# A hybrid Fourier and attention layer on one core: Fourier spectra kept as high and low part, modulation weights fetched two steps ahead, gate pieces between the blocks of the first q

## The chip, the cores and the metric

The kernel runs on 1 core of one Trainium2 chip. The metric is the device time in microseconds (us); a lower number is better. "Before" is the kernel without the change, "after" is the kernel with it. The engines are PE (TensorE, matrix products and transposes), DVE (VectorE), ACT (ScalarE), POOL (GpSimd) and SP (SyncE, which issues most of the DMAs).

## The reference, cut to what matters

One layer for 128 context tokens and 1024 latent tokens: a modulated norm, one input projection whose columns feed three users (a 2-D Fourier transform, windowed attention and two gates), a gated sum, an output projection, then a modulated squared-ReLU MLP. The modulation vectors are a matrix product of their own with `w_ada` (1024 x 6144).

```python
def modulation(cvec, w_ada, b_ada):
    m = jax.nn.silu(cvec) @ w_ada + b_ada
    return [t[:, None, :] for t in jnp.split(m, 6, axis=-1)]

def fourier_mix(u):
    ug = u.astype(jnp.float32).reshape(b, s, N_FOURIER_GROUPS, FOURIER_GROUP_DIM)
    f = jnp.fft.fft2(ug, axes=(1, 3), norm="ortho").real
    return f.reshape(b, s, FOURIER_WIDTH)

def merge_branches(u_f, attn_o, g, w_fo, w_ao, w_out):
    gates = jax.nn.sigmoid(g)
    g_f, g_a = gates[..., :D_MODEL], gates[..., D_MODEL:]
    m = g_f * (fourier_mix(u_f) @ w_fo) + g_a * (attn_o @ w_ao)
    return m @ w_out

def latent_layer(...):
    sh1, sc1, ga1, sh2, sc2, ga2 = mod
    h = rmsnorm(x, g1) * (1 + sc1) + sh1
    u_f, q, k, v, g = split_projection(h, w_in)
    q, k = rope(q), rope(k)
    attn_o = latent_attention(q, k, v, k_ctx, v_ctx, sink)
    x = x + ga1 * merge_branches(u_f, attn_o, g, w_fo, w_ao, w_out)
    h = rmsnorm(x, g2) * (1 + sc2) + sh2
    return x + ga2 * (jnp.square(jax.nn.relu(h @ w_ff1)) @ w_ff2)
```

## The kernel before, in words

Every float32 product is made of three matmuls on a high and a low part of its operands (`mm3`, L192 to L194): high x high, high x low, low x high. A weight block therefore goes three ways before PE can use it: a DMA loads it raw (`wraw`, two buffers), ACT casts the high part (`whi`, three buffers, L144) and DVE subtracts to get the low part (`wlo`, three buffers, L139, a helper line that every subtraction of this kind shares).

The stages, by their place in the span: norm, first modulation and the Fourier input u (to about 120 us); the Fourier transform of the four channel groups, with gate products as filler (to 185); the K and V projection of token tiles 0 to 5 (`tok_proj_round`, L230 to L232, to 210.6); the query projection of the first attention group, `q_pieces(0)`, six pieces of 24 matmuls (to 245); K and V of tiles 6 to 8 (to 258); 36 attention units, four groups of nine 128-token blocks (to about 707); the rest of the Fourier output product (to 729.6); the attention output product `w_ao` with the gated sum (to about 880); the output projection, the second norm and the MLP (to the end).

**Order.** From the K and V projection to the end of attention the order of PE is written out by hand. There PE alternates between attention work (scores `s` L758/L759, transposes `ptp` L792, values `o` L807/L808) and "fill": gate pieces, the query pieces of the next group and three pieces of the Fourier output product (`f_piece`, L929, L950), cut into sub-steps of a few matmuls. `fill_to` spreads the sub-steps evenly over the units. The order on the other engines and in SP's queue is made by a scheduler from the order of the program.

**Banks and buffers.** The fill has two PSUM banks (`mm`), the scores two (`s`), the values one (`o`). A piece of q leaves its bank by two DVE multiplies (L634/L635 for the even half, L637/L638 for the odd half), then DVE rotates (L639, L640), splits, and four stores per block go to `q_d`. The four `qt` tiles have one buffer each, so the multiplies of the next block wait for these stores. A gate piece leaves its bank by one ACT copy to `z` (L661) and one store to `z_d`. The values leave their bank by two ACT copies (`ot`, L816) and two DVE adds (`at`, L817).

**Modulation steps.** The later modulation blocks are worked off in small steps beside all this (`mod_step`). A step loads 128 x 256 of `w_ada` (`mraw`, three buffers, L305), scales it twice on ACT (`mprod`, one buffer, L309) and adds it on POOL (`macc`, L311, 70 times). A block has eight such steps and two more with transposes and sums on DVE (L327, L328); a small matmul with four DVE adds ends it (`mod_fold`, L274, L278). When the block of the first gate vector is complete, `ga_rows` (L1109) stores its columns to DRAM, 4 bytes at a time.

**Fourier output.** The transform stage stores each spectrum raw to `f_d`. At the start of the second last fill piece `load_fx` (L858 to L876) loads the four spectra and the edge rows, and ACT and DVE split them. `load_wfo` (L880 to L892) loads a block of `w_fo` and makes sums (L888) and differences (L889).

## Time and profile before

| | |
|---|---|
| time, median of 3 runs | 1673.37 us (1672.55 to 1673.9) |
| time of the profiled execution | 1677.22 us |
| its span, first to last instruction | 1675.4 us |
| mean granted TensorE clock | 0.993 |
| PE busy | 1618.5 us (97%) |
| DVE busy | 1146.0 us (68%) |
| ACT busy | 902.7 us (54%) |
| POOL busy | 271.4 us (16%) |

The profiled execution took 3.85 us more than the median, and 1.82 us of it lie outside its span. A time stamp in a row of the trace counts from the start of the span. A row reads: start, duration, engine, line, operation, output from inputs, shape; in brackets stands how long the engine was idle before it and what ended this wait. In the rows by stretch each engine has its busy time with the number of its instructions behind it, in the order PE, weight loads, DVE, ACT, POOL, then the granted clock, the busy share of the DMA engines and GB/s.

### The profile page before, as it was taken

What the parts mean: (1) busy time and instruction counts of PE and PEld (TensorE: products, weight loads), DVE (VectorE), ACT (ScalarE), POOL (GpSimd) and SP (SyncE); (2) the same over time, 40 slices, a digit from 0 to 9 for tenths busy, and PEclk for the clock granted to TensorE, in tenths of its full rate; (3) what the DMA queues carried; (4) which work ended last, traced back from release to release, by engine and by line L of the source; (5) the groups of instructions that cost most, each with busy time, mean ns of one, the idle gap of its engine ahead of it and who ended that gap; (6) DMA issues with size and microseconds to landing.
All of it is one profiled execution on the core that took longest, in us unless ns stands there. A gap on an engine that the chain in (4) does not pass through costs nothing.

```text
span 1675.4 us, 24835 instructions
## 1 busy us (share of the span) xinstructions
PE 1618.5 (97%) x8421; PEld 1423.5 (85%) x8421; DVE 1146.0 (68%) x2180; ACT 902.7 (54%) x1743; POOL 271.4 (16%) x368
## 2 busy tenths in 40 slices
PE   6999989998999999899999999999999999999998
PEld 5799888998899999789987888888888888888887
DVE  7653286866767766778648876777776588776764
ACT  7743356776777666455346654444444354444542
POOL 1010243444454333200002400000000100000000
PEclk9999999999999999999999999999999999999999
DMA  8342468555453332498465434544555996656751
GB/s 317 128 131 72 149 209 222 146 91 142 136 142 100 109 93 66 125 298 268 133 214 189 151 106 171 170 151 146 175 143 160 332 377 193 201 189 189 252 162 63
DMA packets 221135, 285.40 MB, mean 170 GB/s; under 512 B 30968, under 2 KB 148664, under 8 KB 220880
## 3 DMA queue, kind: packets, MB, share of 16 engines
q1 hardware_dynamic: 212752, 273.85, 52.0%
q0 software_dynamic: 8256, 9.96, 2.4%
q8 instruction: 66, 1.08, 0.3%
q14 instruction: 61, 0.50, 0.1%
HBM read 205.87 MB, written 77.88 MB: 169 GB/s over the span
## 4 chain that ended last, share of the span: by engine, by line
PE 72%; DVE 5%; DMA 3%; issue 2%; ACT 2%; POOL 1%; SPq 1%; DVEq 0%; ACTq 0%; POOLq 0%
PE x L1848 6%; PE x L1847 6%; PE x L1846 6%; PE x L1450 6%; PE x L1451 6%; PE x L1452 6%; PE mm L192 4%; PE mm L194 4%; PE mm L193 4%; PE ptp L792 2%; PE x L194 2%; PE x L192 2%; PE x L193 2%; PE s L758 2%; PE s L759 2%
## 5 line engine op out<-in xcount | busy, mean ns | idle before, releaser
L139 DVE TENSOR_TENSOR wlo<-wraw,whi 128x1024 fp32r<-128x1024 f32 x109 | 139.3, 1280 | 93.5 <-ACT whi L144 93.3
L144 ACT CAST whi<-wraw 128x1024 fp32r<-128x1024 f32 x107 | 111.8, 1048 | 81.1 <-DMA wraw<-in_w_ff_dram 17.7
L770 ACT ACTIVATE pt<-pt,mx 128x513 f32<-128x513 f32 (+2 forms) x144 | 95.8, 665 | 77.2 <-DVE mx L760 70.6
L193 PE MATMUL mm<-BR,whi 128*128 128x384 f32 x408 | 137.1, 336 | 0.0
L192 PE MATMUL mm<-BR,whi 128*128 128x384 f32 x360 | 129.1, 359 | 4.6 <-DVE qt L635 3.8
L1847 PE MATMUL x<-BR 128*128 128x512 f32 (+1 forms) x348 | 132.9, 382 | 0.0
L1848 PE MATMUL x<-BR 128*128 128x512 f32 (+1 forms) x348 | 132.5, 382 | 0.0
L1846 PE MATMUL x<-BR 128*128 128x512 f32 (+1 forms) x348 | 131.4, 382 | 0.0
L782 POOL TENSOR_SCALAR pt<-pt,mx 128x512 f32<-128x512 f32 (+2 forms) x144 | 97.1, 686 | 184.0 <-DVE mx L780 180.9
L760 DVE CUSTOM_DVE_ANT_0 pt<-s,mask,nsink 128x512 f32<-128x512 f32 (+2 forms) x144 | 96.4, 672 | 42.5 <-PE s L759 40.0
L194 PE MATMUL mm<-BR,wlo 128*128 128x384 f32 x360 | 121.3, 337 | 0.0
L1819 ACT CAST BR<-aa 128x512 fp32r<-128x512 f32 x80 | 49.7, 622 | 105.8 <-PE x L1847 51.3
L311 POOL TENSOR_TENSOR macc<-macc,mprod 128x512 f32<-128x512 f32 x70 | 93.5, 1335 | 40.4 <-ACT mprod L309 32.8
L139 DVE TENSOR_TENSOR pl<-ptp,ph 128x512 fp32r<-128x512 f32 x124 | 83.1, 686 | 19.0 <-ACT ph L795 17.6
L1450 PE MATMUL x<-BR,whi 128*128 128x512 f32 (+2 forms) x204 | 79.3, 389 | 4.1 <-ACT ZR L1474 2.8
L193 PEld LDWEIGHTS mm<-BR,whi 128*128 128x128 f32 x408 | 77.3, 190 | 6.3
L309 ACT ACTIVATE mprod<-mraw,siluc 128x256 f32<-128x256 f32 x140 | 63.8, 504 | 31.6 <-POOL macc L311 27.3
L139 DVE TENSOR_TENSOR BR<-aa,BR 128x512 fp32r<-128x512 f32 x80 | 55.0, 687 | 34.8 <-ACT BR L1819 34.3
L192 PEld LDWEIGHTS mm<-BR,whi 128*128 128x128 f32 x360 | 68.0, 189 | 11.8 <-DVE qt L635 4.4
L1452 PE MATMUL x<-BR,wlo 128*128 128x512 f32 (+2 forms) x204 | 78.0, 383 | 0.0
L1451 PE MATMUL x<-BR,whi 128*128 128x512 f32 (+2 forms) x204 | 78.0, 382 | 0.0
L792 PE MATMUL ptp<-ident,pt 128*128 128x128 f32 x496 | 74.0, 273 | 3.2 <-DVE pl L139 3.2
(450 smaller groups left out, 4758.5 us busy)
## 6 DMA issues: line engine op xcount, KB each, us to landing
aa<-hr_d SPq DMA_DIRECT2D x108, 256.0 KB
ab<-in_w_ff_dram SPq DMA_DIRECT2D x108, 256.0 KB
hr_d<-ZR SPq DMA_DIRECT2D x104, 256.0 KB
wraw<-in_w_in_dram SPq DMA_DIRECT2D x41, 512.0 KB
wraw<-in_w_ff_dram SPq DMA_DIRECT2D x34, 512.0 KB
mraw<-in_w_ada_dram SPq DMA_DIRECT2D x96, 128.0 KB
wraw<-in_w_out_dram SPq DMA_DIRECT2D x24, 512.0 KB
z_d<-z SPq DMA_DIRECT2D x48, 192.0 KB
```

The source lines that it names most:

```text
L139: eng.tensor_tensor(dst, raw, hi.bitcast(F32), ALU.subtract)
L144: nc.scalar.copy(hi, raw)
L192: nc.tensor.matmul(out, ah, bh, start=start, stop=False)
L193: nc.tensor.matmul(out, ah, bl, start=False, stop=False)
L194: return nc.tensor.matmul(out, al, bh, start=False, stop=stop).ins
L792: nc.tensor.transpose(pst[:, h * P : (h + 1) * P], u["pts"][h // 2][:, h % 2, b * P : (b + 1) * P], ident)
L1450: nc.tensor.matmul(po, wh, xh, start=(k == 0 and not cont), stop=False, skip_group_check=cont)
L1451: nc.tensor.matmul(po, wh, xl, start=False, stop=False, skip_group_check=cont)
L1452: nc.tensor.matmul(po, wl, xh, start=False, stop=(k == 3), skip_group_check=cont)
L1846: nc.tensor.matmul(ps, xh, bh, start=start, stop=False, skip_group_check=cont)
L1847: nc.tensor.matmul(ps, xh, bl, start=False, stop=False, skip_group_check=cont)
L1848: nc.tensor.matmul(ps, xl, bh, start=False, stop=stop, skip_group_check=cont)
```

## The change

The change does these things:

1. The transform stage splits each spectrum on the spot and stores high and low part (`f_d` has twice the size). `load_fx` loads both parts straight into their slots: eight DMAs, no cast, no subtraction. The edge rows of `w_fo` are split in the transform stage too and go through `wex_d`; the matmul of the edge rows has 12 rows and no longer 96.
2. The raw weights of modulation steps are loaded two steps ahead in the K and V projection and in attention (`mod_raw`, `raw_ahead`), with four buffers in place of three; `mprod` has two buffers in place of one; `z` has two in place of three.
3. Two gate pieces are taken out of the fill of attention and put behind the second and the fourth piece of the first q (`front`). The fill of attention has 53 pieces in place of 55 and is 16 sub-steps (48 matmuls) shorter.
4. Weight blocks in attention follow a plan (`at`): raw load 16 sub-steps before the piece that needs them, split 8 sub-steps before. Before, both were called for at the start of the piece before. The `w_fo` blocks 0 and 2 have places of their own in the plan.
5. In attention `mod_fold` takes its PSUM bank from the ring of the scores and not from that of the fill.
6. In `f_piece` the DVE difference leaves out column 0, which an ACT copy writes alone; the buffers of all pieces inside attention are the same pair.
7. The 24 loads of the attention output (`att_d`) in front of `w_ao` go to POOL's queue and no longer to SP's.
8. Many small steps go through `defer`, which would hold them back for some slots of the hand-written order. `lag` is `False` throughout, and then `defer` runs them at once.

```diff
+    fold_bank = [mmt]
...
+    def mod_raw(blk, k):
+        b0 = 2 * D // MB
+        n = (blk - b0) * 8 + k
+        while raw_next[0] <= max(n, min(n + raw_ahead[0], raw_end[0] - 1)):
...
+            nc.sync.dma_start(wa, w_ada[kk * P : (kk + 1) * P, b * MB : (b + 1) * MB])
+            raw_next[0] += 1
+        return raw_got.pop(n)
...
-                    f = p2.tile([P, FC], F32, tag="f", name=nm("f"), bufs=2)
-                    nc.scalar.copy(f[:, 0:512], lat)
-                    nc.scalar.copy(f[:, 512:FC], bc[:, o : o + 130])
-                    nc.sync.dma_start(f_d[2 * i + gi // 2], f)
+                    for r, src in ((slice(0, 512), lat), (slice(512, FC), bc[:, o : o + 130])):
+                        nc.scalar.copy(fh[:, r], src)
+                        sub(nc.vector, fl[:, r], src, fh[:, r])
+                    for e_, f in enumerate((fh, fl)):
+                        nc.sync.dma_start(f_d[2 * i + gi // 2, e_], f.bitcast(F32))
...
+        lag, slots_, later = [False], [0], []
+        def defer(n, fn):
+            if lag[0]:
+                later.append((slots_[0] + n, fn))
+            else:
+                fn()
...
+            front = [gate_piece(*gate_ids[48 - len(gates) + n], front_w(n)) for n in range(2)]
+            for n, piece in enumerate(q_pieces(0)):
                 for _ in piece:
                     pass
+                if n in (1, 3):
+                    for _ in front.pop(0):
+                        pass
...
         def load_fx():
-            wfo.append(load_wfo(0))
             for i in range(4):
-                raw = raw_w([P, FC])
-                nc.sync.dma_start(raw, f_d[i])
-                hi, lo = (slot(2 * i + e)[:, 0:FC] for e in range(2))
-                nc.scalar.copy(hi, raw)
-                sub(nc.vector, lo, raw, hi)
-                fx.append((hi, lo))
+                hl = [slot(2 * i + e)[:, 0:FC] for e in range(2)]
+                for e in range(2):
+                    nc.sync.dma_start(hl[e].bitcast(F32), f_d[i, e])
+                fx.append(tuple(hl))
...
-            nc.vector.tensor_tensor(o[:, 0:512], psx, y, ALU.subtract)
+            nc.vector.tensor_tensor(o[:, 1:512], psx[:, 1:512], y[:, 1:512], ALU.subtract)
...
+            k = KC * first[b]
+            at(k - 16, lambda w=w: raw_load(w))
+            at(k - 8, lambda w=w: raw_split(w))
...
+        at(NP8 - 16, load_fx)
...
+        for m, k in ((0, NP8 - 24), (2, NP8 - 4)):
+            put(m, k, lambda _, m=m: wfo_load(m))
+            put(m, k + 8, wfo_sums)
+            put(m, k + 10, wfo_split)
...
         def fill_steps():
-            for n, (pc, b, q) in enumerate(pieces_):
-                for w in blocks_[: b + 2]:
-                    fetch(w)
-                if n == FX_AT:
-                    load_fx()
+            for pc, b, q in pieces_:
...
+        fold_bank[0] = lambda: q1.tile([P, 512], F32, tag="s", name=nm("s"), bufs=2)
...
-                z = zload(att_d[m], j)
+                z = zload(att_d[m], j, nc.gpsimd)
```

**The first q on DVE.** These are DVE's rows from the end of the first q block to the middle of the second, in the kernel before. `mm_353` ends the first block, `mm_356` begins the second; `mtr` and `red` belong to a modulation block, `qr` to the K projection.

```order
L637 TENSOR_TENSOR qt_354_2106<-mm_353_2081,ropet_1605 128x384
L638 TENSOR_TENSOR qt_355_2108<-mm_353_2081,ropet_1605 128x384
L689 TENSOR_TENSOR qr_341_2032<-ra_342_2033,rb_343_2034 128x4x32x2
L639 TENSOR_TENSOR qt_348_2071<-qt_348_2071,qt_354_2106 128x384
L640 TENSOR_TENSOR qt_349_2073<-qt_349_2073,qt_355_2108 128x384
L139 TENSOR_TENSOR qt_348_2071<-qt_348_2071,qt_354_2106 128x384
L139 TENSOR_TENSOR qt_349_2073<-qt_349_2073,qt_355_2108 128x384
L634 TENSOR_TENSOR qt_357_2145<-mm_356_2120,ropet_1605 128x384
L327 STREAM_TRANSPOSE mtr_290_1782<-macc_264_1686 128x256
L635 TENSOR_TENSOR qt_358_2147<-mm_356_2120,ropet_1605 128x384
L328 TENSOR_REDUCE red_289_1781<-mtr_290_1782 128x8
L327 STREAM_TRANSPOSE mtr_291_1785<-macc_264_1686 128x256
```

The same place in the kernel after (`mm_361` ends the first block, `mm_369` begins the second; between them PE works on the gate piece `mm_367`):

```order
L674 TENSOR_TENSOR qt_362_2136<-mm_361_2111,ropet_1631 128x384
L741 TENSOR_TENSOR ra_350_2063<-x_284_1753,rope_1643 128x256
L743 TENSOR_TENSOR rb_351_2064<-x_284_1753,rope_1643 128x256
L675 TENSOR_TENSOR qt_363_2138<-mm_361_2111,ropet_1631 128x384
L676 TENSOR_TENSOR qt_356_2101<-qt_356_2101,qt_362_2136 128x384
L744 TENSOR_TENSOR qr_349_2062<-ra_350_2063,rb_351_2064 128x4x32x2
L677 TENSOR_TENSOR qt_357_2103<-qt_357_2103,qt_363_2138 128x384
L141 TENSOR_TENSOR qt_356_2101<-qt_356_2101,qt_362_2136 128x384
L141 TENSOR_TENSOR qt_357_2103<-qt_357_2103,qt_363_2138 128x384
L141 TENSOR_TENSOR wlo_377_2255<-wraw_375_2252,whi_376_2254 128x1024
L659 TENSOR_TENSOR qt_370_2209<-mm_369_2184,ropet_1631 128x384
L660 TENSOR_TENSOR qt_371_2211<-mm_369_2184,ropet_1631 128x384
```

The transposes and sums no longer stand between the first multiplies of the second block. Between the two blocks now stands the low part of the weights for the second gate piece (`wlo_377`).

**SP's queue in attention.** These are SP's rows from the stores of the gate vector (`ga_d`) on, in the kernel before.

```order
L1109 DMA ga_d_81<-mods_91 128x8x1 x2
L662 DMA z_d_74<-z_682_3732 128x384
L739 DMA qT_701_3812<-q_d_71 32x4x384 x4
L305 DMA mraw_709_3845<-in_w_ada_dram 128x256
L305 DMA mraw_722_3901<-in_w_ada_dram 128x256
L820 DMA att_d_72<-at_691_3769 128x128 x2
L305 DMA mraw_735_3965<-in_w_ada_dram 128x256
```

The same place in the kernel after, from three rows ahead of the stores:

```order
L303 DMA mraw_720_3915<-in_w_ada_dram 128x256
L892 DMA att_d_72<-at_668_3692 128x128 x2
L717 DMA z_d_75<-z_675_3726 128x384
L1078 DMA wraw_909_4774<-in_w_in_dram 128x8x128
L1236 DMA ga_d_82<-mods_92 128x8x1 x2
L799 DMA qT_714_3888<-q_d_71 32x4x384 x4
L303 DMA mraw_722_3921<-in_w_ada_dram 128x256
L892 DMA att_d_72<-at_701_3839 128x128 x2
```

One load of modulation weights that stood behind the stores now stands ahead of them, and the raw load of a weight block has moved ahead of them as well.

**ACT at the same place.** In the kernel before, ACT multiplies the weights `mraw_709` between the two copies of one unit's values (`ot_719`).

```order
L816 COPY ot_719_3882<-o_705_3828 64x256
L309 ACTIVATE mprod_710_3847<-mraw_709_3845,siluc_90 128x256 x2
L795 CAST ph_725_3915<-ptp_724_3910 128x512
L770 ACTIVATE pt_712_3862,mx_713_3863<-pt_712_3862,mx_713_3863 128x385
L816 COPY ot_719_3882<-o_705_3828 64x256
L840 CAST kth_2401<-ptp_727_3922 128x512
L309 ACTIVATE mprod_723_3903<-mraw_722_3901,siluc_90 128x256 x2
```

In the kernel after, the values of that unit are `ot_727`:

```order
L883 COPY ot_727_3948<-o_718_3904 64x256 x2
L861 CAST ph_733_3981<-ptp_732_3976 128x512
L832 ACTIVATE pt_724_3935,mx_725_3936<-pt_724_3935,mx_725_3936 128x385
L716 COPY z_735_3988<-mm_713_3884 128x384
L323 ACTIVATE mprod_731_3969<-mraw_720_3915,siluc_91 128x256 x2
L916 CAST kth_2499<-ptp_736_3991 128x512
L323 ACTIVATE mprod_749_4043<-mraw_722_3921,siluc_91 128x256 x2
```

Both copies now stand ahead of the modulation step, and this step uses the load that stands ahead of the stores of `ga_d`.

More of the change, by code (lines that the diff above doesn't have):

```diff
@@ L517, in pad @@
             return dhi[:, r], dlo[:, r]
+        wx = p2.tile([4, D], F32, name="wx")
+        nc.sync.dma_start(wx, w_fo.rearrange("(g c) n -> g c n", g=4)[:, 64])
+        wxh, wxl = (p2.tile([4, D], F32R, name=nm("wx")) for _ in range(2))
+        nc.scalar.copy(wxh, wx)
+        sub(nc.gpsimd, wxl, wx, wxh)
+        for k, x in enumerate((wxh, wxh, wxl)):
+            nc.sync.dma_start(wex_d[k], x.bitcast(F32))
         for gi in range(4):
@@ L795, in out_t @@
             nc.scalar.copy(ph, pst)
-            sub(nc.vector, pl, pst, ph)
             u["p"][b] = ph, pl
+            defer(PL_LAG, lambda: sub(nc.vector, pl, pst, ph))
         def out_v(u, b):
@@ L921, in f_piece @@
         def f_piece(m):
-            if m % 2 == 0 and m + 2 < KC:
-                wfo.append(load_wfo(m + 2))
+            while fbank[0] is not mmt and len(wfo) < min(4, m // 2 + 2):
+                wfo.append(load_wfo(2 * len(wfo)))
             out = []
@@ L997, in backbone_kernel, with at, raw_load, raw_split @@
         FX_AT = len(pieces_) - 2
-        qdone = {(0, j) for j in range(NJ)}
         done = [0]
-        def fill_steps():
-            for n, (pc, b, q) in enumerate(pieces_):
-                for w in blocks_[: b + 2]:
-                    fetch(w)
-                if n == FX_AT:
-                    load_fx()
+        plan = {}
+        def at(k, fn):
+            plan.setdefault(max(0, k), []).append(fn)
+        def raw_load(w):
+            raw = w[1]["raw"] = raw_w([P, KC, P])
+            nc.sync.dma_start(raw, w_in[:, w[0] : w[0] + P].rearrange("(k p) n -> p k n", p=P))
+        def raw_split(w):
+            raw = w[1].pop("raw")
+            hi = wp.tile([P, KC, P], F32R, tag="whi", name=nm("whi"), bufs=3)
+            lo = wp.tile([P, KC, P], F32R, tag="wlo", name=nm("wlo"), bufs=3)
+            w[1][0] = hi, lo
+            nc.scalar.copy(hi, raw)
+            defer(2, lambda: sub(nc.vector, lo, raw, hi))
+        first = {}
+        for n, (_, b, _) in enumerate(pieces_):
+            first.setdefault(b, n)
+        for b, w in enumerate(blocks_):
+            if 0 in w[1]:
+                continue
+            k = KC * first[b]
+            at(k - 16, lambda w=w: raw_load(w))
+            at(k - 8, lambda w=w: raw_split(w))
+        NP8 = KC * len(pieces_)
+        at(NP8 - 16, load_fx)
+        held = {}
+        def put(m, k, f):
+            def go():
+                held[m] = f(held.get(m))
+            at(k, go)
+        def wfo_split(xy):
+            hi = wp.tile([P, 4, 256], F32R, tag="whi", name=nm("whi"), bufs=3)
+            lo = wp.tile([P, 4, 256], F32R, tag="wlo", name=nm("wlo"), bufs=3)
+            nc.scalar.copy(hi, xy)
+            defer(2, lambda: sub(nc.vector, lo, xy, hi))
+            wfo.append((hi, lo))
+        for m, k in ((0, NP8 - 24), (2, NP8 - 4)):
+            put(m, k, lambda _, m=m: wfo_load(m))
+            put(m, k + 8, wfo_sums)
+            put(m, k + 10, wfo_split)
+        def fill_steps():
+            for pc, b, q in pieces_:
                 for _ in pc:
                     yield
-                if q is not None:
-                    qdone.add(q)
                 yield
@@ L1054, in unit_order @@
             out = []
+            ts = [lambda b=b: out_t(prev, b) for b in range(nb)]
             for h in range(4):
@@ L1058, in unit_order @@
                     out += [lambda v=late.pop(0): out_v(*v), None]
-            for b in range(nb):
-                out += [lambda b=b: out_t(prev, b), None]
+            for f in ts:
+                out += [f, None]
             late += [(prev, b) for b in range(nb)]
@@ L1094, in backbone_kernel @@
         out_v(pending, 0)
+        tick(3)
+        lag[0] = False
+        fold_bank[0] = mmt
+        assert not later and not plan
         man.close()
         fold_auto[0] = True
+        raw_ahead[0] = 0
         mod_step(len(msteps) - MOD_B)
@@ L1179, in backbone_kernel @@
                 nc.scalar.copy(mh, zv)
[L1180 to L1181 removed]
+                ins = sub(nc.vector, ml, zv, mh)
+                with tc.issue_after(ins.ins):
+                    mod_step(min(MOD_2, len(msteps) - MOD_LATE))
         mod_step(len(msteps) - MOD_LATE)
```

165 lines of the change are left out of this document (99 added, 66 removed).

## The prediction

> **What bounds the kernel now.** I read the page's engine totals first, then the list of what PE waited for, and then the rows around each of its large waits between 200 and 745 us, since the change touches little outside that stretch.
>
> ```profile
> PE 1618.5 (97%) x8421; PEld 1423.5 (85%) x8421; DVE 1146.0 (68%) x2180; ACT 902.7 (54%) x1743; POOL 271.4 (16%) x368
> PE o L807 <- DVE at L817: 6.1, 5, 4.4
> PE mm L192 <- DVE qt L635: 3.8, 2, 3.1
> PE x L192 <- ACT ER L1158: 3.2, 2, 2.1
> PE ptp L792 <- DVE pl L139: 3.2, 3, 1.9
> PE mm L929 <- ACT pt L940: 1.4, 1, 1.4
> 270.00:700.00 430.00, 415.82 (x2410) 384.79 (x2409) 308.08 (x741) 297.56 (x687) 187.29 (x283) 0.99 0.45 120
> ```
>
> PE is busy 97% of the span, so PE bounds the kernel, and the change keeps its matmuls: both orders hold the same 7888 rows. Only PE's idle time and its clock can be won or lost. In attention (last row) PE is busy 415.82 of 430 us, DVE 308.08, ACT 297.56: 14.2 us of idle time there, and two engines with a quarter of their time free. The waits in the list are few and large, and the change aims at each of them.
>
> **The first q.** These are three PE rows and one DVE row of that place; the bracket is the wait ahead of the row. The last row is DVE's and PE's load by stretch, just ahead of it.
>
> ```profile
> 219.76 0.44 PE L192 MATMUL mm<-BR,whi 128*128 128x384 f32 x1 [0.65 <-DVE qt L635]
> 224.93 0.44 PE L192 MATMUL mm<-BR,whi 128*128 128x384 f32 x1 [0.71 <-DVE qt L638]
> 232.47 0.45 PE L192 MATMUL mm<-BR,whi 128*128 128x384 f32 x1 [3.11 <-DVE qt L635]
> 231.06 0.56 DVE L634 TENSOR_TENSOR qt<-mm,ropet 128x384 f32<-128x384 f32 x1 [2.67 <-DMA q_d<-qt]
> 208.00:216.00 8.00, 8.00 (x44) 7.53 (x43) 7.86 (x15) 5.02 (x12) 4.46 (x5) 1.00 0.69 226
> ```
>
> PE loses 0.65 + 0.71 + 3.11 = 4.47 us. DVE is full (7.86 of 8) with the K and V work, so it leaves the first q bank late; then its multiplies for the second block wait for the stores of the first out of the single `qt` buffers. The first gate piece now gives PE 24 matmuls at just that place. PE did 44 matmuls in the 8 us row, 0.18 us each, so a piece is 4.4 us of work that needs no `qt` tile: more than the 3.11 us wait. The first wait stays, and grows by the two modulation sums that the order puts ahead of the first multiplies. I leave 1 us of idle time there and take a gain of **3.5** (bounds 1 and 4.5). New here is that the second gate piece's weights sit in a third `whi` buffer while the last K and V round runs, which has two left: 0 to 1.7 us, in the sum of small costs below.
>
> **The stall at 378.** Now the largest: PE, ACT, SP, then the DMA traffic from 366 to 374 and from 374 to 382, then three stretches.
>
> ```profile
> 382.43 0.77 PE L807 MATMUL o<-ph,vg 128*128 128x512 f32 x1 [4.42 <-DVE at L817]
> 378.85 0.91 ACT L309 ACTIVATE mprod<-mraw,siluc 128x256 f32<-128x256 f32 x2 [3.35 <-DMA mraw<-in_w_ada_dram]
> 362.40 1.00 SPq L1109 DMA_DIRECT2D ga_d<-mods  x2
> 367.78 6.99 SPq L305 DMA_DIRECT2D mraw<-in_w_ada_dram  x2
> DMA packets 284, 0.25 MB, mean 32 GB/s; under 512 B 119, under 2 KB 284, under 8 KB 284
> DMA packets 2601, 1.99 MB, mean 249 GB/s; under 512 B 320, under 2 KB 2599, under 8 KB 2599
> 368.00:376.00 8.00, 8.00 (x48) 7.44 (x47) 6.42 (x14) 7.13 (x17) 5.00 (x7) 1.00 0.76 85
> 376.00:384.00 8.00, 3.58 (x17) 2.98 (x16) 3.10 (x9) 4.89 (x12) 4.42 (x7) 0.83 1.05 258
> 384.00:392.00 8.00, 8.00 (x38) 7.46 (x37) 3.49 (x11) 4.60 (x12) 3.99 (x6) 0.75 0.83 191
> ```
>
> The root is not the modulation step but the gate vector's stores at 362.40, written 4 bytes at a time: behind them the DMA engines move 32 GB/s for eight microseconds, then 249. The weights asked for at 367.78 reach ACT at 378.85. ACT works in order, so the second half of the value copies stands behind the step, and PE waits 4.42 us for its `o` bank. The clock falls too: 17 matmuls in 3.58 us, then 38 in 8.00, where the row before had 48 in 8.00. At that rate these took 2.83 and 6.33 us, so 0.75 + 1.67 = 2.4 us are lost beside the wait. The change leaves the stores where they are. But the step that ACT reaches there now uses a load issued ahead of them, and both copies stand ahead of the step. The load behind the stores is used one step later; counting ACT's rows of the new order from 375.5 by their durations, ACT gets there about 379, when it has landed. Gain **6.8** (4.42 + 2.4; bounds 2 and 6.8).
>
> The Trainium skill, "TensorE: Matmul & The Clock Gate", Part 1, says that the clock halves after an idle window of about 3.4 us. The trace agrees on the 3.11 us wait of the first q (clock 1.00 there) and on this one; not on the tail below, where no wait reaches 2 us. By that rule the clock loss of the tail would not go with its waits, and the sum would be about 1.3 us smaller.
>
> **The end of attention.** PE and DVE rows, then ACT's idle time for the raw spectra, then two stretches.
>
> ```profile
> 671.51 0.66 PE L792 MATMUL ptp<-ident,pt 128*128 128x128 f32 x4 [1.93 <-DVE pl L139]
> 685.02 0.50 PE L807 MATMUL o<-ph,vg 128*128 128x512 f32 x1 [0.53 <-DVE at L817]
> 687.93 0.33 PE L758 MATMUL s<-kth,qT 128*128 128x128 f32 x1 [1.04 <-DVE mx L760]
> 696.09 0.50 PE L808 MATMUL o<-pl,vg 128*128 128x512 f32 x1 [0.95 <-DVE pl L139]
> 699.30 1.22 PE L929 MATMUL mm<-BR,whi 128*128 128x512 f32 x2 [1.41 <-ACT pt L940]
> 694.02 0.69 DVE L888 TENSOR_TENSOR wraw<-wraw 128x512 f32<-128x512 f32 x1 [0.81 <-DVE at L817]
> L858 ACT CAST BR<-wraw 128x642 fp32r<-128x642 f32 x4 | 2.9, 732 | 3.2 <-DMA wraw<-f_d 3.2
> 696.00:704.00 8.00, 6.50 (x22) 5.27 (x23) 4.39 (x8) 2.59 (x6) 0.46 (x1) 0.67 0.71 202
> 712.00:720.00 8.00, 8.00 (x47) 6.93 (x46) 5.14 (x12) 4.24 (x11) 0.00 (x0) 1.00 0.87 277
> ```
>
> The 1.93 us at 671 come from the split of the spectra: DVE's subtractions stand behind ACT's casts, and these wait 3.2 us for DMA. After the change neither cast nor subtraction is there. Gain **1.9** (bounds 0 and 1.9). The same split costs the transform stage eight subtractions, at most 8 x 0.69 = 5.5 us of DVE (the `L888` row, of the same width); there the filler covers them: 0, at most 1.
>
> The four waits from 685 to 699 sum to 3.93 us, and 22 matmuls took 6.50 us where 47 took 8.00 (3.74 for 22): 2.76 more by the clock, 6.7 in all. DVE is freed of the split, the wait for `L940` is partly undone since the difference no longer covers column 0, and the sums of the second `w_fo` block have a planned place. But the later `w_fo` blocks still fall into this stretch, with a cast of 1 us ahead of such copies. I take a little under half: **3** (bounds 0 and 6.7).
>
> **Into `w_ao`.** Two PE waits, what ACT waited for from 700 to 760, one stretch, and the loads that POOL issues already.
>
> ```profile
> 734.55 0.62 PE L192 MATMUL x<-ER,whi 128*128 128x384 f32 x2 [2.09 <-ACT ER L1158]
> 741.67 0.44 PE L192 MATMUL x<-ER,whi 128*128 128x384 f32 x1 [1.12 <-ACT ER L1158]
> ACT ER L1158 <- DMA z<-att_d: 18.7, 11, 4.0
> 744.00:752.00 8.00, 8.00 (x48) 8.00 (x47) 4.99 (x10) 7.17 (x14) 0.00 (x0) 1.00 1.00 339
> L831 POOL DMA_DIRECT2D vg<-vh_d x4: 963/1024/1167, 270.1 to 493.7; - x4
> ```
>
> PE loses 3.2 us because the attention output comes back late. POOL is idle there, so its queue can issue these loads without the stores of the Fourier product ahead of them. Against it: a POOL issue took 1.02 us, 24 of them 25 us, and the DMA engines are full (1.00, 339 GB/s). I take half, **1.5** (bounds -3 and 3.2; the lower end if the 24 issues set the pace). The Trainium skill, "DMA: Bandwidth & Descriptors", "Issuing engines are not separate DMA queues", says that all queues run on the same 16 engines and that spreading only saves issue time. The full DMA row agrees; by it this term would be near 0.
>
> **New costs.** The fill of attention is 16 sub-steps, 48 matmuls at 0.18 us or 8.6 us, shorter. Of its 14.2 us of idle time, 4.42 + 1.93 + 3.93 are explained above; 3.9 are many small waits. With less fill and the same attention work DVE goes from 72% to about 73% of the stretch. I expect small waits of the same size once more: 4. The fold in the scores' ring, two `z` buffers and two weight buffers in the last K and V round get 1 together. Costs **5** (bounds 0 and 12). The `defer` steps cost and gain nothing while `lag` is false. Two `mprod` buffers spare ACT waits that PE hardly sees: 0.
>
> Sum: 3.5 + 6.8 + 1.9 + 3 + 1.5 - 5 = **11.7 us**. The profiled execution (1677.22) would come to 1665.5; it ran 3.85 above the median, 1.82 of it outside its span. The waits are tied to the order of the work, so I take the sum off the median: 1673.37 - 11.7 = **1661.7**.
>
> **Rivals.**
>
> *Weights too late (slower).* Splits now start 8 sub-steps ahead of use, where the call came a whole piece ahead. With 53 pieces and three Fourier pieces in 430 us a sub-step is about 1 us.
>
> ```profile
> L144 ACT CAST whi<-wraw 128x1024 fp32r<-128x1024 f32 x19 | 19.9, 1049 | 5.4 <-PE mm L193 2.7 <-POOL wraw L891 2.7
> L139 DVE TENSOR_TENSOR wlo<-wraw,whi 128x1024 fp32r<-128x1024 f32 x20 | 25.0, 1251 | 3.7 <-ACT whi L144 3.6
> ```
>
> A split takes 1.05 + 1.25 = 2.3 us, so it decides once the queues on ACT and DVE delay it by over 5.7 us. If 17 splits come 1.2 us late, that is 20 us: 1673.37 - 11.7 + 20 = 1682. For it: one late load held ACT for 3.35 us. Against: no cast here waited for its own DMA, and both engines have slack. Chance 0.12.
>
> *The fill leaves holes (no change).* If attention's own chain, not PE, sets its length, the 8.6 us of fill taken out come back as idle time: 1661.7 + 8.6 = 1670.3, with some lost clock 1672. For it: DVE waits at every unit. Against: PE is 97% busy there. Chance 0.12.
>
> *The stall moves one step.* If the load behind the `ga_d` stores is still late, ACT stands still one step later, with less behind it: the gain of 6.8 becomes 2, 1666.5. Chance 0.16.
>
> *POOL's loads land later.* The 3.2 us become 6.2: the term is -3, 1666.2. Chance 0.10.
>
> **How the numbers follow.** The forecast has 0.50, from 1655 to 1668. A measurement here tells about 0.2% (3.3 us) from no change. Faster (below 1670.0): 0.50 + 0.16 + 0.10 less 0.02 for mixtures, 0.74. Within: 0.12 and 0.01 of them, 0.13. Slower (above 1676.7): 0.12 and 0.01, 0.13. With all terms at their upper bounds and no costs the sum is 23.1, 1650.3. The range goes from 1650 to 1676: it takes in the holes and leaves out the late weights.
>
> **What would show it.** Right: the wait of `mm` for `qt` below 1.5 us in all; no wait of over 2 us for the `o` bank after the `ga_d` stores, the clock at 1.00 behind them; nothing for the spectra on ACT or DVE near the end of attention. Wrong: PE waiting for `whi` or `wlo` in attention; ACT waiting for `mraw` again; more than 10 us of small waits between 270 and 690; the waits ahead of `w_ao` above 5 us.

## The result and the profile after

The kernel after took 1663.87 us (median of 4 runs, 1662.33 to 1667.19) against 1673.63 us before on the same chip: a ratio of 0.9945, 95% interval 0.9928 to 0.9963, or 9.8 us less. The forecast was 1661.7 with a range from 1650 to 1676. The profiled executions are further apart than the medians, 1677.22 and 1662.33 us, since the one of before is slower than all four runs timed beside after, and the one of after is the fastest of its four. Their spans differ by 14.9 us, and what follows accounts for these 14.9; some 5 of them belong to these two executions and not to the medians.

The engine totals of after, what its PE waited for from 185 to 730 us, and the two stretches in which before had lost its clock:

```profile
PE 1616.5 (97%) x8421; PEld 1419.2 (85%) x8421; DVE 1141.1 (69%) x2181; ACT 896.9 (54%) x1737; POOL 284.4 (17%) x391
```

```profile
PE ptp L858 <- DVE pl L141: 3.5, 3, 2.3
PE o L873 <- DVE at L887: 2.1, 3, 1.1
PE s L818 <- DVE mods L281: 1.8, 3, 1.1
PE mm L194 <- ACT z L716: 1.3, 2, 0.9
PE o L874 <- DVE pl L141: 0.9, 1, 0.9
PE mm L194 <- DVE qt L660: 0.6, 1, 0.6
PE x L233 <- DVE wlo L141: 0.3, 1, 0.3
```

```profile
360.00:380.00 20.00, 19.53 (x124) 18.25 (x123) 13.34 (x39) 15.07 (x40) 10.08 (x16) 1.00 0.49 88
380.00:400.00 20.00, 19.85 (x115) 18.32 (x113) 15.68 (x42) 16.54 (x41) 13.02 (x18) 1.00 0.79 203
680.00:700.00 20.00, 20.00 (x108) 15.82 (x107) 10.63 (x20) 8.71 (x21) 6.69 (x13) 1.00 0.73 227
700.00:720.00 20.00, 20.00 (x105) 15.56 (x105) 15.79 (x28) 13.73 (x36) 6.99 (x13) 1.00 0.92 301
```

The same four stretches of before:

```profile
360.00:380.00 20.00, 18.01 (x110) 16.58 (x108) 11.26 (x33) 13.36 (x34) 9.62 (x17) 1.00 0.78 99
380.00:400.00 20.00, 17.57 (x84) 16.16 (x85) 12.11 (x33) 13.20 (x32) 9.36 (x13) 0.83 0.62 152
680.00:700.00 20.00, 16.07 (x100) 13.44 (x99) 17.02 (x35) 12.57 (x32) 7.05 (x17) 0.97 0.42 129
700.00:720.00 20.00, 20.00 (x102) 16.94 (x100) 10.12 (x25) 6.48 (x17) 0.00 (x0) 0.86 0.66 198
```

Every wait of over 2.4 us that before had between 200 and 745 us is gone, no wait for `ER` is left, and the clock is at 1.00 in every 20 us from 180 to 760. What is left are small waits, 10.7 us of PE in all from 185 to 730, where before had 20.4. One sign that the prediction named for being wrong did come, ACT waiting for `mraw`, once, and PE waits nowhere behind it:

```profile
391.84 0.91 ACT L323 ACTIVATE mprod<-mraw,siluc 128x256 f32<-128x256 f32 x2 [1.21 <-DMA mraw<-in_w_ada_dram]
```

One thing moved against the change and does not show as a wait: PE is busy in each of the last two stretches of after for all 20 us, yet does little. That is the matmul of the edge rows, which now has 12 rows. Here are rows of one Fourier piece of after, then the same two kinds of matmul in a kernel that has 96 rows again (`x_rows96`, below):

```profile
700.07 0.62 PE L999 MATMUL x<-BR,whi 128*128 128x512 f32 x2
700.53 0.39 PE L999 MATMUL x<-BR,wlo 128*128 128x512 f32 x1
700.85 0.50 PE L999 MATMUL x<-BR,BT 12*128 12x512 f32 x1
701.27 0.55 PE L1020 MATMUL x<-BR,whi 128*128 128x130 f32 x3
```

```profile
703.53 0.39 PE L1000 MATMUL x<-BR,wlo 128*128 128x512 f32 x1
703.76 0.40 PE L1000 MATMUL x<-BR,BT 96*128 96x512 f32 x1
703.99 0.45 PE L1021 MATMUL x<-BR,whi 128*128 128x130 f32 x3
```

Read the starts. With 96 rows the three follow each other at 0.23 us; with 12 rows the distances are 0.32 and 0.42. No bracket stands there, since PE counts as busy.

### The profile page after: what moved, and what is told of

Same layout as the page of the kernel before. It is cut to its first block, busy times and chain, and to the rows that moved or that the text cites. A ratio compares the mean times of both kernels' runs of the same rounds, so it can differ in the third digit from the quotient of the medians.

```text
span 1660.5 us, 24885 instructions
## 1 busy us (share of the span) xinstructions
PE 1616.5 (97%) x8421; PEld 1419.2 (85%) x8421; DVE 1141.1 (69%) x2181; ACT 896.9 (54%) x1737; POOL 284.4 (17%) x391
## 4 chain that ended last, share of the span: by engine, by line
PE 76%; DVE 6%; ACT 2%; issue 1%; DMA 1%; SPq 0%; POOL 0%; DVEq 0%; ACTq 0%
PE x L1976 6%; PE x L1974 6%; PE x L1975 6%; PE x L1578 6%; PE x L1580 6%; PE x L1579 6%; PE mm L194 4%; PE mm L196 4%; PE mm L195 4%; PE ptp L858 3%; PE x L196 2%; PE x L194 2%; PE x L195 2%; PE s L818 2%; PE s L819 2%; PE o L873 2%
## 5 line engine op out<-in xcount | busy, mean ns | idle before, releaser
L146 ACT CAST whi<-wraw 128x1024 fp32r<-128x1024 f32 x88 | 91.9, 1049 | 91.2 <-DMA wraw<-in_w_ff_dram 18.2
L195 PEld LDWEIGHTS mm<-BR,whi 128*128 128x128 f32 x408 | 77.0, 189 | 6.0
L861 ACT CAST ph<-ptp 128x512 fp32r<-128x512 f32 x124 | 70.6, 586 | 12.6 <-PE ptp L858 11.3
L194 PE MATMUL mm<-BT,whi 128*128 128x384 f32 x216 | 76.5, 354 | 0.0
```

Of the source, the lines that this page charges most:

```text
L194: nc.tensor.matmul(out, ah, bh, start=start, stop=False)
L195: nc.tensor.matmul(out, ah, bl, start=False, stop=False)
```

## The experiments

Each kernel was timed in five rounds against the kernel before on the same chip, and is given as a ratio to it; 0.001 is 1.7 us. "After" stands at 0.9945. It was not timed again with these kernels, and three chips were used for them: one for the first four, one for `b_garow`, `x_foldmm`, `x_oldplan` and `x_rawspec`, one for the rest. Before has medians of 1675.1 to 1676.7 us there and of 1673.6 us beside after. So a distance to after, or between two of these chips, that is not well above the half width of the intervals (0.0011 to 0.0018) says little. Two kernels are before with one part of the change or one edit, the others are after with one part undone or one edit; all compute the whole reference.

**The edge rows on 96 rows again** (`x_rows96`)

```diff
-        wx = p2.tile([4, D], F32, name="wx")
+        wx = p2.tile([96, D], F32, name="wx")
+        nc.gpsimd.memset(wx, 0.0)
...
-                    nc.sync.dma_start(ex[4 * k + 2 * r : 4 * k + 2 * r + 2], f_d[2 + r, k % 2][0:65:64])
+                    nc.sync.dma_start(ex[32 * k + 2 * r : 32 * k + 2 * r + 2], f_d[2 + r, k % 2][0:65:64])
```

> The kernel after, with the edge rows of the Fourier product spread over 96 rows again (zero weights in the rows between), and nothing else changed. In the trace of after, the interval from a 12-row matmul to its neighbours is longer than for a full one: 0.32 and 0.42 us where 512 columns take 0.23, 0.21 and 0.25 where 130 columns take 0.11, about 0.6 us for a Fourier piece. Theory: the few rows cause it, eight pieces make 4.7 us, so the time falls from 1663.9 to about 1659, and the five pieces behind attention take 22.2 us again in place of 25.3. Rival: the pieces are slower for another reason (banks, copies, loads that arrive late), then the time stays at 1663.9 within 1 us and the five pieces at 25 us.

Measured: 0.9907 (0.9893 to 0.992), 0.0038 or 6.4 us below after by the ratio; the medians, 1661.1 and 1663.87 us, are 2.8 us apart. The five pieces behind attention go from 692.2 to 714.4 us, 22.2 us; in after from 692.9 to 718.5, 25.6 us. The theory holds for the matmuls. Two waits for `ER` (0.63 and 2.16 us) came back, probably since the shorter pieces cover less of the loads, and from 720 to 740 us the clock is at 0.91, a loss of 0.09 x 17.84 = 1.6 us. These take most of the gain in the profiled execution, whose span is 1660.0 us where that of after is 1660.5. What the rows cost PE is measured; what mending them gives in time lies between 2.8 and 6.4 us by the medians and the ratio.

**The loads of the attention output on SP's queue** (`x_spload`)

```diff
-                z = zload(att_d[m], j, nc.gpsimd)
+                z = zload(att_d[m], j)
```

> The kernel after, with the 24 loads of the attention output on SP's queue again. Theory of the prediction: SP's queue made these loads late, so PE's waits for ER in front of the attention output product come back, 2 to 3.2 us, 1666 to 1667. Rival: the DMA engines, full there in before, have been relieved by the rest of the change or by the earlier end of attention; then the waits stay away and the time is 1663.9 within 1 us.

Measured: 0.9973 (0.9962 to 0.9984), 0.0028 or 4.7 us above after; the two intervals just touch. The size is above the theory's and the mechanism is another. ACT's casts wait for the loads again, but PE waits for none of them. PE's loss stands later: these are PE's row and one of the DVE rows ahead of it.

```profile
761.01 0.40 PE L277 MATMUL mm<-red,quads 128*128 128x16 f32 x2 [4.35 <-DVE red L342]
751.64 0.56 DVE L1301 TENSOR_TENSOR z<-z,z 128x384 f32<-128x384 f32 x1 [1.34 <-DMA z<-part_d]
```

The modulation fold has a fixed place in PE's order there, and DVE comes to its sums late, behind gate products whose loads came late out of SP's queue. That the late loads caused it is read from the rows, and not tried by itself. The spans are 7.8 us apart: this wait, 1.7 us of clock behind it (0.91 from 760 to 780), and 1.6 us of clock from 420 to 440, far ahead of these loads. When the loads are issued is plain: POOL issues the first at 682.9 us in after, while stores of the attention output still run; SP issues it at 697.4 here, half a microsecond behind the last of these stores, and at 710.9 in before. So 14.5 of the 28 us between before and after come with the queue. A POOL issue took 0.54 us and not the 1.02 us that the prediction bounded it with.

**The two gate pieces back in attention** (`x_nofront`)

```diff
-            front = [gate_piece(*gate_ids[48 - len(gates) + n], front_w(n)) for n in range(2)]
...
-        gate_left = gate_ids[50 - len(gates) :]
+        gate_left = gate_ids[48 - len(gates) :]
```

> The kernel after, with the two gate pieces back in the fill of attention. Theory of the prediction: the wait of 3.1 us for the qt buffers in the first q comes back, and the denser attention had cost about 4 us of small waits that go again, so the time moves little: 1662 to 1666, with the first q at 4 to 4.5 us of PE idle time (after: 2.0) and attention at 4 to 5 (after: 8.4). Rival: the small waits in attention have another cause (the fold in the scores' ring, the order of DVE) and stay, then the time is about 1666.5.

Measured: 0.9957 (0.9944 to 0.9969), 2.0 us above after, with intervals that overlap. PE's waits in the first q:

```profile
221.76 0.44 PE L194 MATMUL mm<-BR,whi 128*128 128x384 f32 x1 [1.16 <-DVE qt L660]
235.56 0.69 PE L194 MATMUL mm<-BR,whi 128*128 128x384 f32 x1 [4.87 <-DVE qt L660]
```

The wait came back, larger than before: 6.0 us against 2.0 in after. So the front pieces are worth some 4 us of PE's time at their place. In attention PE waits 8.3 us in all against 8.4, but the waits are others. The 2.31 us of after and its three waits for the fold (1.84 us) are not there, and 3.3 us stand at the place of the old stall, where a modulation step is between two value copies again and waits for POOL's add:

```profile
374.02 0.47 PE L869 MATMUL o<-ph,vg 128*128 128x512 f32 x1 [1.14 <-DVE mx L816]
383.84 0.47 PE L869 MATMUL o<-ph,vg 128*128 128x512 f32 x1 [2.12 <-DVE at L883]
380.18 0.91 ACT L323 ACTIVATE mprod<-mraw,siluc 128x256 f32<-128x256 f32 x2 [1.26 <-POOL macc L325]
```

Without these two the small waits are 5.0 us, where the theory had 4 to 5. So this kernel does not decide whether the shorter fill made the small waits grow: with the fill, the order of the work on DVE and ACT changed as well.

**The prefetch alone, on the kernel before** (`b_prefetch`; `mod_raw` as in the change)

```diff
-    MRB = [3, 1]
+    MRB = [4, 1]
...
-                        wa = mraw_tile()
-                        nc.sync.dma_start(wa, w_ada[k * P : (k + 1) * P, blk * MB : (blk + 1) * MB])
+                        wa = mod_raw(blk, k)
```

> The kernel before with one part of the change: modulation weights loaded two steps ahead, four buffers. Theory of the prediction: the stall of 4.42 us at the gate vector's stores goes, with its clock loss of 2.4, so 1673.6 becomes about 1667, and ACT waits nowhere for mraw in attention. Rival: the load that stands behind the stores is late whichever step uses it, then ACT waits for mraw one step later, PE's wait for the o bank keeps 2 us or more, and the time is 1671 to 1673.

Measured: 0.9958 (0.9944 to 0.9971), 7.0 us below before. PE's wait for the `o` bank and ACT's wait of the step behind it:

```profile
380.17 0.47 PE L819 MATMUL o<-ph,vg 128*128 128x512 f32 x1 [1.77 <-DVE at L829]
380.77 0.51 ACT L320 ACTIVATE mprod<-mraw,siluc 128x256 f32<-128x256 f32 x1 [1.13 <-DMA mraw<-in_w_ada_dram]
```

The size is the forecast one, but not all of it stands at the stall. There, 4.42 - 1.77 = 2.65 us of the wait and the clock loss of 3.0 us are gone; the waits of 1.31 and 0.28 us at the start of attention are gone too, here as in the next kernel, and why was not found. The stall is not wholly gone: the step is still between the two copies here, and ACT does wait one step later, 1.13 us, as the rival had it, but with little behind it.

**The gate vectors stored by rows, on the kernel before** (`b_garow`)

```diff
-            nc.sync.dma_start(ga_d[row + tok].rearrange("(m p) -> p m", p=P), mods[:, k * 8 : k * 8 + 8, tok])
+            nc.tensor.transpose(pg[0:8, 0:P], mods[:, k * 8 : k * 8 + 8, tok], ident)
+            nc.vector.tensor_copy(gs, pg[0:8, 0:P])
+            nc.sync.dma_start(ga_d[row + tok].rearrange("(m p) -> m p", p=P), gs)
```

> The kernel before, with one edit that the change does not have: the gate vectors are transposed on PE first and stored by rows of 512 bytes, and no longer 4 bytes at a time. Theory: the 4-byte stores are the root of the stall in attention; without them the modulation weights arrive in time although they are asked for as late as before, the wait of 4.42 us for the o bank and the clock loss behind it go, and the time falls by 6 to 7 us, a ratio of about 0.996, like that of the kernel with the prefetch alone (0.9958). Rival: the weights are late because they are asked for too late; then the wait stays and the ratio is 0.999 to 1.001.

Measured: 0.9974 (0.9962 to 0.9986), 4.4 us below before, between the two. ACT and PE at the place of the stall:

```profile
375.28 0.91 ACT L309 ACTIVATE mprod<-mraw,siluc 128x256 f32<-128x256 f32 x2 [1.38 <-POOL macc L311]
378.87 0.47 PE L807 MATMUL o<-ph,vg 128*128 128x512 f32 x1 [2.47 <-DVE at L817]
```

ACT no longer waits for a DMA, so the stores were what made the weights late. But it waits 1.38 us for POOL's add (one `mprod` buffer), still with the second value copies behind it, and PE keeps 2.47 of its 4.42 us. The stall had two causes: the slow stores, and a modulation step that stands between two copies for which PE waits.

**The fold in the fill's banks** (`x_foldmm`)

```diff
-        fold_bank[0] = lambda: q1.tile([P, 512], F32, tag="s", name=nm("s"), bufs=2)
```

> The kernel after, with the fold of the modulation blocks in the fill's PSUM banks again. Theory: the scores' waits for the fold's adds (0.26, 0.47 and 1.11 us, three times in after) go, and what the fill's banks wait for in their place is less (0.55 us once in before): the time falls by 1 to 2 us, a ratio to before of 0.9935 against 0.9945. Rival: the adds delay the fill by as much; the ratio stays at 0.9945 within 0.0005.

Measured: 0.9926 (0.9913 to 0.994). The three waits of the scores for the fold's adds (1.84 us) are gone, and one of 0.57 us of the fill stands in their place. The intervals of this kernel and of after overlap, so the traces show the 1.3 us and the times do not settle it.

**Weight blocks called for as before** (`x_oldplan`)

```diff
-            k = KC * first[b]
-            at(k - 16, lambda w=w: raw_load(w))
-            at(k - 8, lambda w=w: raw_split(w))
+            k = KC * first[b - 1] if b else 0
+            at(k, lambda w=w: raw_load(w))
+            at(k, lambda w=w: raw_split(w))
```

> The kernel after, with weight blocks in attention called for at the start of the piece before, load and split together, as before the change; the plan for the two blocks of w_fo stays. Theory: the splits at 8 sub-steps fall on DVE at places where it is full (a wait of 2.31 us at 430 us stands behind the subtraction of one); with the earlier call the small waits in attention fall from 8.4 to about 5 us, and the ratio from 0.9945 to about 0.9925. Rival: DVE is as full wherever the splits fall; waits of the same sum stand elsewhere, and the ratio stays within 0.001 of 0.9945.

Measured: 0.9938 (0.9925 to 0.9951), the rival's. The waits in attention stand at the same places with the same sizes; the largest, 2.01 us here, still follows a weight subtraction. Here are DVE's rows ahead of it in after:

```profile
427.36 0.40 DVE L342 TENSOR_REDUCE red<-mtr 128x8 f32<-128x256 f32 x1
427.68 1.30 DVE L141 TENSOR_TENSOR wlo<-wraw,whi 128x1024 fp32r<-128x1024 f32 x1
428.91 0.43 DVE L341 STREAM_TRANSPOSE mtr<-macc 128x256 f32<-128x256 f32 x1
429.27 0.65 DVE L141 TENSOR_TENSOR pl<-ptp,ph 128x512 fp32r<-128x512 f32 x1
```

```profile
429.97 0.66 PE L858 MATMUL ptp<-ident,pt 128*128 128x128 f32 x4 [2.31 <-DVE pl L141]
```

PE needs the last of these rows, and DVE does three others first. When the split is written into the program did not decide here where DVE does it.

**Raw spectra again** (`x_rawspec`: the kernel with 96 rows, the store of `f_d` and its split in `load_fx` as before the change, `load_fx` three sub-steps later so that two raw buffers are enough; the edge rows of `w_fo` are still split in the transform stage)

```diff
-                hl = [slot(2 * i + e)[:, 0:FC] for e in range(2)]
-                for e in range(2):
-                    nc.sync.dma_start(hl[e].bitcast(F32), f_d[i, e])
+                raw = raw_w([P, FC])
+                nc.sync.dma_start(raw, f_d[i, 0])
+                hi, lo = (slot(2 * i + e)[:, 0:FC] for e in range(2))
+                nc.scalar.copy(hi, raw)
+                sub(nc.vector, lo, raw, hi)
...
-        at(NP8 - 16, load_fx)
+        at(NP8 - 13, load_fx)
```

> The kernel after with 96 edge rows, and with the spectra stored raw and split on ACT and DVE near the end of attention again; compared with the same kernel without this (ratio 0.9907). Theory of the prediction: the split's wait of 1.9 us at the transposes comes back, and a part of the waits and the clock loss in the last units, 3 to 6 us in all: a ratio of 0.993 to 0.994. Rival: those waits went because the w_fo blocks have planned places and fewer pieces stand in the fill; then the ratio stays within 0.001 of 0.9907.

Measured: 0.9889 (0.9875 to 0.9902), not above the kernel it is compared with (0.9907). Near the end of attention PE waits 0.75, 0.33 and 0.69 us where that kernel waits 0.53; no wait for `ER` is left. The theory falls: taking the split of the spectra out of attention's end is not what removed before's waits there. The 0.75 and 0.69 us stand behind DVE's sums of `w_fo` blocks (669.78 and 679.92 us), not behind a split. The 1.93 us at 671 do not come back, but this kernel does not test them: they stand behind the split of the edge rows of `w_fo`, as the next section shows, and that one was not put back.

**The load of the split spectra three sub-steps later** (`x_rows96_late`)

```diff
-        at(NP8 - 16, load_fx)
+        at(NP8 - 13, load_fx)
```

> The kernel after with 96 edge rows and the load of the spectra three sub-steps later; it stands between the two kernels with 96 rows that were run (0.9907 with split spectra, 0.9889 with raw spectra loaded three sub-steps later and two waits of 2.16 and 0.63 us for ER less). Theory: the waits for ER hang on where the loads of the spectra fall in SP's queue and on the bytes they move, not on the split; with the later place the ratio falls to about 0.989. Rival: storing the split spectra itself costs, by twice the bytes, 1.3 MB more in and out; then the ratio stays at 0.9907 within 0.0007 and the waits for ER stay.

Measured: 0.9923 (0.991 to 0.9936), and a wait for `ER` of 2.08 us. The ratio is above both forecasts, though its interval meets that of `x_rows96`. The first load was issued 1.7 us later (647.4 for 645.7 us), and the theory falls: the place of the load does not explain the difference to raw spectra. That storing the split spectra itself costs is what is left of the two, and not shown; what it would cost, and through which queue, was not found. The loads of the spectra are issued by 657 us in `x_rows96`, 60 us ahead of the `ER` waits, and the two last kernels below, with raw spectra, have such waits as well (0.75 and 1.66 us).

**The deferred steps switched on** (`x_lag`)

```diff
         base, pending, late = 16.0, None, []
+        lag[0] = True
```

> The kernel after with the machinery of deferred steps switched on from the first attention unit on: subtractions, rotations and value copies are written into the program one to six slots later. It was forecast to cost and gain nothing while it is off. Theory: DVE's order, not its load, makes the small waits in attention (8.4 us in after, the largest 2.31 behind a weight subtraction); later places for steps that nobody waits for let the transposes' subtractions go first, and the small waits fall to about 5 us: a ratio of 0.992 to 0.993 against 0.9945. Rival: the scheduler orders DVE by its own estimate of times whatever the program's order, or a later rotation holds the fill's bank; then 0.9945 within 0.001, or above.

Measured: 0.9935 (0.9924 to 0.9947), within 0.001 of after, with the same waits in attention (2.32, 1.05, 1.11, 0.89, 0.85 us). Writing steps later does not move them in time here, as with the weight splits.

**The parts together** (`x_best`: raw spectra, 96 rows, the fold in the fill's banks; the edits of `x_rawspec` and `x_foldmm`), **and with the stores by rows** (`x_best_garow`, where the transposed rows lie in a raw weight buffer):

```diff
+            gs = raw_w([8, P])
```

> The kernel after with three parts undone or mended: 96 edge rows, raw spectra split at the end of attention, the fold in the fill's banks. The single edits gave 0.9889 (the first two) and 0.0019 less than after (the third). If the parts add, the ratio is 0.987; if the fold's gain is hidden by other small waits, 0.989.

Measured: 0.9897 (0.9884 to 0.991). The fold's 1.3 us do not add to a measurable gain. This kernel and `x_rawspec` (0.9889) are the fastest of the study, and their intervals, like that of `x_rows96`, lie wholly below that of after (0.9945).

> The same kernel with the gate vectors stored by rows of 512 bytes. In the kernel before this gave a ratio of 0.9974; in after the prefetch already takes the modulation weights past the slow stores. Theory: both mend the same stall, so nothing more is won: 0.987 within 0.001. Rival: the 4-byte stores still delay z stores and the next group's keys in attention, and the second pair of them delays the MLP's; then 0.985.

Measured: 0.9958 (0.9945 to 0.9971), 10 us worse than without the stores by rows. PE's new waits:

```profile
814.78 0.27 PE L1241 MATMUL mm<-ident,mods 128*8 128x128 f32 x1 [1.07 <-DVE mods L281]
820.71 2.93 PE L1417 MATMUL x<-whi,BR 128*128 128x512 f32 x6 [5.65 <-ACT whi L146]
```

The buffer that the transposed rows take is missing for a weight block of the output product: the second raw load of `w_out` is issued at 816.24 us, behind the stores at 814.98, and in `x_best` at 796.29. And the fold ahead of the transposes is waited for. So the edit has a cost of its own here, and whether the slow stores still hurt the kernel after stays open.

## Why the prediction was right, and where its steps were not

The span's 14.9 us by place, from the two traces; "idle" is PE's waits, "clock" the time lost by the rows of 20 us above (busy time by one less the clock). The forecast was made for the medians, which moved 9.8 us, so the measured column is some 5 us too large for it as a whole. The clock rows are the least certain: with most of the waits of the last units left, the two kernels built on before (`b_prefetch`, `b_garow`) have a clock of 0.91 and 1.00 in the two stretches where before has 0.97 and 0.86.

| place | forecast | measured | how |
|---|---|---|---|
| first q | 3.5 | 2.2 | idle 4.47, after 1.96 + 0.31 |
| stall at 378 | 6.8 | 7.4 | idle 4.42 to 0; clock 0.17 x 17.57 = 3.0 |
| wait at 671 | 1.9 | 1.9 | idle 1.93 to 0 |
| last units | 3 | 7.2 | idle 3.93 to 0; clock 0.03 x 16.07 + 0.14 x 20 = 3.3 |
| into `w_ao` | 1.5 | 3.2 | idle 3.2 to 0 |
| start of attention | - | 1.75 | idle 1.31 + 0.28 + 0.16 to 0 |
| small waits | -5 | -4.5 | idle 3.9 to 8.4 |
| 12-row matmuls | - | -5.4 | 8 pieces of (25.6 - 22.2) / 5 = 0.68 |
| sum | 11.7 | 13.8 | span: 14.9 |

**The first q.** Right in mechanism: the wait comes back as soon as the pieces go (`x_nofront`). What stays is 2.0 and not 1.0 us: the two gate pieces' own copies of `z` on ACT hold the bank for 0.44 and 0.88 us, which the prediction did not price. The first wait did not grow in this execution (0.65, then 0.64 us); in most kernels of the study with this part of the change it is 0.9 to 1.7 us.

**The stall.** Right in size by the trace (7.4); the prefetch alone gives 7.0 on the chip, of which its trace puts 5.7 at this place. "The root is not the modulation step but the gate vector's stores" was half of it: with fast stores 2.47 us of the wait stay, and POOL's add and the place of the step between the copies are the other half. The change meets the second half by another order of ACT and the first by the earlier load. That order is not safe: in `x_nofront`, which has the earlier load and both `mprod` buffers, the step is between two copies again and PE waits 2.12 us. The "0" for the second `mprod` buffer was not tried by itself. The rival that the stall moves one step came without its price: ACT waits 1.21 us for `mraw` later, and PE does not.

**The end of attention.** The sum was too small, and "The 1.93 us at 671 come from the split of the spectra" named the wrong split. These are the rows of before ahead of that wait:

```profile
668.90 0.62 ACT L875 CAST BT<-wraw 96x512 fp32r<-96x512 f32 x1
669.03 0.68 DVE L139 TENSOR_TENSOR BR<-wraw,BR 4x512 fp32r<-4x512 f32 x1 [0.60 <-ACT BR L875]
669.64 1.09 DVE L139 TENSOR_TENSOR BT<-wraw,BT 4x512 fp32r<-4x512 f32 x1
670.76 0.69 DVE L139 TENSOR_TENSOR pl<-ptp,ph 128x512 fp32r<-128x512 f32 x1
```

PE needs the last row, and ahead of it DVE subtracts the four edge rows of `w_fo` behind ACT's casts of them (L875). The last subtraction of a whole spectrum ended at 663.2 us. `b_prefetch` and `b_garow`, which keep this split, wait 1.57 and 1.51 us at the same place behind the same two rows. The change takes the edge rows of `w_fo` out of attention too, so the gain of 1.9 came, from a part of the first item of the change that the prediction did not name. It is read from the rows of three kernels and was not tried by itself.

Of the last units' 6.7 us all went, where the prediction took under half. Which part of the change did it was not tried by itself either. The rows point to the planned places of the `w_fo` blocks: the 0.95 us at 696 stand behind DVE's sums of one (from 694.02), and in after the sums of two blocks are done at 663 and 672 us, with one wait of 0.38 us (at 676) behind them.

The rule of the clock gate ("TensorE: Matmul & The Clock Gate", Part 1, of the Trainium skill) had been weighed there: by it the clock loss of the tail would stay with no long wait to remove. In after the clock is at 1.00 there and the waits, of 1.4 us and less, are gone, so these two traces speak against that reading of the rule.

**Into `w_ao`.** Right in direction, and larger. The rule that spreading DMAs over issuing engines only saves issue time ("DMA: Bandwidth & Descriptors", "Issuing engines are not separate DMA queues", of the Trainium skill) would have this term near 0. It is 3.2 in the trace, and undoing it costs 4.7 by the ratio. The loads start 14.5 us earlier than out of SP's queue in the same kernel, because POOL does not stand behind the stores of the attention output. What is saved is the time of standing in SP's queue and not the time of the issues (0.54 us each on POOL, 0.43 on SP), so the rule does not settle this term. But PE's loss in `x_spload` was no wait for these loads, so that the 3.2 us went by this part of the change alone is not shown.

**New costs.** 4.5 of the 5 came. Whether the reason was "With less fill" stays open, since `x_nofront` with the longer fill has 5.0 us of small waits and 3.3 at the old stall. In after 1.84 us are the fold's. The others did not move with the weight plan or with the deferred steps, and the prefetch alone leaves them at 4.3; what makes them is not settled.

**What was missed.** The 12 rows, listed in the change as a mere detail, cost 5.4 us by the trace, with the three pieces inside attention taken at the price of the five behind it, and mending them gave 2.8 to 6.4 us in the time of `x_rows96`. The rival of late weights did not come: from 185 to 730 us PE waits for `whi` or `wlo` only once, 0.31 us in the last K and V round. The holes did not come either: PE is as full in attention as before.

That the sum came so close is luck: two errors of some 5 us met. The end of attention and the way into `w_ao` gave 4 to 6 us more than forecast, and the edge rows took 5.4 that were not forecast.

## What to carry to other kernels

A wait is worth more than its length where the clock falls behind it, so read the clock of the stretches after it before pricing it. When a wait stands behind a split, look at the shape in the row to see which split it is. When a load is late, look for what its queue had to finish first: here it was 8 KB written 4 bytes at a time. And a matmul with fewer rows is not a smaller matmul: price it from the start-to-start distances of its neighbours, not from its columns.

## What the runs showed of the hardware

**Few rows cost more.** A matmul of 12 rows between matmuls of 128 takes PE 0.32 + 0.42 us from start to start for 512 columns with its neighbours, where 96 rows take 0.23 + 0.23. These are the groups by form of the two kernels, with the mean duration in ns:

```profile
L999 PE MATMUL x<-BR,BT 12*128 12x512 f32 x4 | 2.0, 497 | 0.0
L1020 PE MATMUL x<-BR,BT 12*128 12x130 f32 x4 | 1.3, 322 | 0.0
```

```profile
L1000 PE MATMUL x<-BR,BT 96*128 96x512 f32 x4 | 1.6, 395 | 0.0
L1021 PE MATMUL x<-BR,BT 96*128 96x130 f32 x4 | 1.1, 276 | 0.0
```

The Trainium skill, "TensorEngine Tiling (Array Packing)", Key Properties, says that a change of tiling mode drains TensorE. The rows agree with a drain on either side of the 12-row matmul, some 0.1 and 0.2 us; that 12 rows change the mode and 96 do not is an inference from these two cases alone.

**Four-byte stores slow what follows.** Two stores of 4 KB, written 4 bytes at a time, were issued at 362.40 us; 2077 packets passed from 362 to 366, and then all 16 DMA engines together moved 32 GB/s from 366 to 374. With rows of 512 bytes (`b_garow`) it was 141 GB/s in these eight microseconds, and ACT had no wait for a DMA at that place:

```profile
DMA packets 1154, 1.12 MB, mean 141 GB/s; under 512 B 128, under 2 KB 1153, under 8 KB 1153
```

**The same wait does not always cost clock.** The wait of 2.0 to 2.4 us near 430 stands in after and in nine kernels of the study. In three of these ten the clock fell behind it. Here are the 20 us around it of `x_lag`, with a wait of 2.32 us, and then of `x_best`, with 2.44:

```profile
420.00:440.00 20.00, 17.68 (x93) 16.14 (x92) 16.57 (x37) 12.86 (x27) 7.10 (x8) 0.91 0.32 100
```

```profile
420.00:440.00 20.00, 17.56 (x101) 16.08 (x101) 17.98 (x39) 14.20 (x30) 7.33 (x9) 1.00 0.34 106
```

The Trainium skill, "TensorE: Matmul & The Clock Gate", Part 1, says that the gate's window runs freely, so that the same kernel can come out differently from run to run; these rows agree with that. The rule of the idle window of about 3.4 us, which the prediction took from there, does not cover them: the waits are 2.0 to 2.4 us, and in three kernels the clock fell. By an estimate from the mean clocks, the clock is also much of the spread between executions of after: 1662.33 us at 0.997, 1667.19 at 0.995, and 0.002 of 1661 us is 3.3 of these 4.9.
